# Softmax with logits of the other sign and the sink as a 129th column; output projections by 512 columns

## The chip, the cores and the metric

One NeuronCore of a Trainium2 chip runs the whole program in one launch. The metric is the device time of that launch in microseconds (us); lower is better. Its engines are TensorE (PE, matmuls; its weight loads are listed as PEld), VectorE (DVE), ScalarE (ACT), GpSimd (POOL) and SyncE (SP, which here only issues DMAs). Each takes its instructions in one fixed order and waits at the first that isn't ready.

## The reference

A decoder trunk of two layers over 1,024 positions of width 1,024, in float32. Layer A is a gated DeltaNet with an output projection (2,048 x 1,024). One set of keys and values (4 heads of 64) is then computed, and layer B is an attention of 32 query heads over a window of 128 positions, with an output projection of the same size. What the change touches is the softmax of layer B, whose denominator has one more term, a learned sink for each head, and the two products `@ w_out`:

```
q = rms_norm(q, q_gain) * (64 ** -0.5)
logits = einsum("bnqkgd,bnskd->bnkgqs", q, k_band) + bias
logits = where(mask, logits, -inf)            # 128 of 256 keys of a band lie in the window
m = maximum(max(logits), sink)
p = exp(logits - m)
probs = p / (sum(p) + exp(sink - m))
o = einsum("bnkgqs,bnskd->bnqkgd", probs, v_band)
return (o * silu(z)) @ w_out
```

## The kernel before

Each float32 operand of a large product is split into a rounded part and a remainder (hi and lo), and a product is three matmuls: hi by hi, hi by lo, lo by hi. TensorE's order is that in which the code is written; the orders of DVE, ACT, POOL and SP are made by a scheduler from priorities.

**Weights.** They stream through `wraw`, two buffers of 512 KB. `take()` hands out the next weight and fetches the ones ahead; `weight()` lets SP issue the load, then has POOL copy it into `whi` (L150; for weights with a norm gain POOL multiplies the gain in, two L153, and ACT rounds, L155), and DVE forms the remainder `wlo` in two halves (L157). `weights()` yields the sources in the order of use.

**Output projection** (`out_proj`, called for layer A with `a_w_out` and for layer B with `b_w_out`). It goes over two halves of 512 positions, two halves `cp` of 512 output columns, and in each over the 16 slices k of 128 input rows, four by four (k4). The stationary operand is the transposed activation (`oh` its rounded part, `ol` its remainder), the moving one the weight. Four accumulators in PSUM, one for each 128 positions, take 48 products each. A weight tile holds four slices k of 256 columns, so each accumulator is filled in two halves b. `tick()` counts steps: small pieces of other work, such as the transposes of the next norm (L239, which need the normed rows `xo` of DVE's L232), are written into PE's order at given ticks (`later(15, ...)` for the first half). `og_load` loads the next rows of activations, and DVE's L895 forms their remainder `ol`.

**Attention** (`b_attend`, between the projections). There are 64 blocks: 8 groups of 4 heads, each with 8 blocks of 128 queries. For block i PE's order has, in turns with the matmuls of the following groups' q and z products (L971 to L973 and L180 to L184): `turn(i)`, the transposes of its probabilities (L1192); `q_turn(i + 3)`; `logits(i + 2)`; `values(i - 1)`. So the softmax of a block has about the time of two blocks on PE before its `turn`. `logits` lets PE form the products with the keys (L1166, L1167), DVE put the window's 128 logits together (L1168), add the bias and take the running maximum from the sink on (L1172), negate it (L1176) and subtract it from the sink (L1178); ACT takes the exp of the sink's term (L1179) and of the logits, with their sum (L1182); DVE adds the sink's term (L1184) and inverts (L1185); POOL multiplies (L1186). POOL also makes the rounded queries (L1137) and masks the transposed probabilities (L1197), DVE norms the queries (L1103 among others).

## Time and profile before

| | |
|---|---|
| median of 3 runs | 1890.71 us (1887.74 to 1893.08) |
| profiled execution, its own time | 1894.54 us |
| span of its instructions | 1892.8 us |
| mean granted TensorE clock | 0.995 |
| busy: PE, DVE, ACT, POOL | 97%, 65%, 44%, 27% |

The profile is taken from one execution; its time lies a little above the median of the runs. The stages that the change touches are the projection of layer A (899 to 1089 us of the span), the attention (1170 to 1704) and the projection of layer B (1704 to 1893). Matmuls overlap, so the distance of two starts is what a matmul costs in a stream, not its own duration. The granted clock is given as a share of full speed: 1.00 is 2.4 GHz, 0.50 is 1.2 GHz.

### The profile page before, as it was taken

The page shows a single profiled execution, that of the slowest core. Times are in us where ns is not written, and L with a number is a line of the kernel's source. Part 1 is how long each engine was busy: PE and PEld are TensorE (multiplying, and loading weights), DVE is VectorE, ACT ScalarE, POOL GpSimd, SP SyncE. Part 2 cuts the span into 40 slices and gives each one's busy share as a digit, 9 for nine tenths or more (in the row PEclk, how much of TensorE's full clock was granted, in tenths as well). Part 3 has the DMA queues.
Part 4 walks back from the last instruction along what each step waited for, and adds up shares of the span by engine and source line. Part 5 has one row for each costly group of instructions (what it writes and reads, how often), then busy time and mean ns, then how long its engine had stood idle before and what let it go on. Part 6 is the DMA issues. An engine that isn't in the chain of part 4 may idle for free.

```text
span 1892.8 us, 34012 instructions
## 1 busy us (share of the span) xinstructions
PE 1829.7 (97%) x13186; PEld 1567.2 (83%) x13186; DVE 1239.6 (65%) x3014; ACT 838.1 (44%) x1968; POOL 512.6 (27%) x581
## 2 busy tenths in 40 slices
PE   6999999999999998999999999999999999999999
PEld 5667777787878776778999999888788788879999
DVE  6677776868595878765545366787776776753432
ACT  6446353635445364423011043656756666771100
POOL 0222222322232223221211232333433333321211
PEclk9999999999999999999999999999999999999999
DMA  4611111111111111133654321111211111226542
GB/s 149 143 37 34 56 45 57 34 56 46 34 57 34 46 34 58 33 96 99 229 182 152 112 90 46 42 38 46 67 32 48 56 49 43 73 73 200 188 166 82
DMA packets 151270, 149.74 MB, mean 79 GB/s; under 512 B 7242, under 2 KB 124484, under 8 KB 151108
## 3 DMA queue, kind: packets, MB, share of 16 engines
q1 hardware_dynamic: 140768, 130.40, 22.2%
q10 hardware_dynamic: 10340, 17.16, 2.9%
q8 instruction: 104, 1.70, 0.4%
q14 instruction: 58, 0.48, 0.1%
HBM read 116.05 MB, written 31.49 MB: 78 GB/s over the span
## 4 chain that ended last, share of the span: by engine, by line
PE 68%; DVE 13%; issue 5%; ACT 4%; POOL 3%; DMA 1%; POOLq 0%; ACTq 0%; SPq 0%; DVEq 0%
PE mm L182 8%; PE mm L180 8%; PE mm L184 8%; PE acc L920 6%; PE acc L919 6%; PE acc L921 6%; PE mm L971 4%; PE mm L973 3%; PE mm L972 3%; DVE acc L494 3%; PE pv L1213 2%; DVE wlo L157 2%; PE tp L1192 1%; PE kqp L666 1%; PE lg L1167 1%
## 5 line engine op out<-in xcount | busy, mean ns | idle before, releaser
L180 PE MATMUL mm<-hh,whi 128*128 128x512 f32 (+1 forms) x1040 | 427.2, 411 | 2.6 <-ACT hh L246 2.5
L182 PE MATMUL mm<-hl,whi 128*128 128x512 f32 (+1 forms) x1040 | 417.3, 401 | 1.6 <-DVE hl L247 1.5
L184 PE MATMUL mm<-hh,wlo 128*128 128x512 f32 (+1 forms) x1040 | 415.1, 399 | 0.0
L157 DVE TENSOR_TENSOR wlo<-wraw,whi 128x512 fp32r<-128x512 f32 x292 | 210.8, 749 | 239.4 <-POOL whi L150 214.0
L150 POOL TENSOR_SCALAR whi<-wraw 128x1024 fp32r<-128x1024 f32 x110 | 121.8, 1107 | 493.2 <-PE acc L921 248.3
L180 PEld LDWEIGHTS mm<-hh,whi 128*128 128x128 f32 x1040 | 197.5, 190 | 38.1 <-issue 4.6
L184 PEld LDWEIGHTS mm<-hh,wlo 128*128 128x128 f32 x1040 | 197.1, 190 | 36.0 <-issue 4.2
L182 PEld LDWEIGHTS mm<-hl,whi 128*128 128x128 f32 x1040 | 197.5, 190 | 34.6 <-issue 4.2
L971 PE MATMUL mm<-whi,hh 128*128 128x256 f32 x608 | 179.9, 296 | 0.0
L494 DVE SCALAR_TENSOR_TENSOR acc<-u,cw,acc 128x512 f32<-128x512 f32 x192 | 160.8, 839 | 23.5 <-POOL acc L491 21.0
L973 PE MATMUL mm<-whi,hl 128*128 128x256 f32 x608 | 171.8, 283 | 0.0
L972 PE MATMUL mm<-wlo,hh 128*128 128x256 f32 x608 | 171.7, 282 | 0.0
L919 PE MATMUL acc<-whi,hh 128*128 128x256 f32 x512 | 145.0, 283 | 0.0
L920 PE MATMUL acc<-wlo,hh 128*128 128x256 f32 x512 | 144.9, 283 | 0.0
L921 PE MATMUL acc<-whi,hl 128*128 128x256 f32 x512 | 144.9, 283 | 0.0
L971 PEld LDWEIGHTS mm<-whi,hh 128*128 128x128 f32 x608 | 115.6, 190 | 10.9 <-issue 10.8
L1182 ACT ACTIVATE lsb<-lsb,nm 128x128 f32<-128x128 f32 x256 | 99.8, 392 | 54.6 <-DVE se L1178 44.4
L972 PEld LDWEIGHTS mm<-wlo,hh 128*128 128x128 f32 x608 | 115.8, 190 | 0.2
L973 PEld LDWEIGHTS mm<-whi,hl 128*128 128x128 f32 x608 | 115.5, 190 | 0.0
L920 PE MATMUL acc<-wlo,oh 128*128 128x256 f32 x384 | 108.7, 283 | 1.2 <-DVE wlo L157 1.2
L919 PE MATMUL acc<-whi,oh 128*128 128x256 f32 x384 | 108.6, 283 | 0.0
L921 PE MATMUL acc<-whi,ol 128*128 128x256 f32 x384 | 108.5, 283 | 0.0
(355 smaller groups left out, 4207.0 us busy)
## 6 DMA issues: line engine op xcount, KB each, us to landing
wraw<-in_a_w_in SPq DMA_DIRECT2D x48, 512.0 KB, 4.0
wraw<-in_a_w_out SPq DMA_DIRECT2D x32, 512.0 KB, 4.2
wraw<-in_b_w_in SPq DMA_DIRECT2D x32, 512.0 KB, 4.0
wraw<-in_b_w_out SPq DMA_DIRECT2D x32, 512.0 KB, 3.9
og<-zs SPq DMA_DIRECT2D x32, 256.0 KB, 2.0
ogT<-zs SPq DMA_DIRECT2D x24, 256.0 KB, 2.1
btab<-lt SPq DMA_DIRECT2D x1, 4096.0 KB, 24.2
dm<-gd SPq DMA_DIRECT2D x8, 512.0 KB, 3.7
```

Of the source, the lines that this page charges most:

```text
L150: nc.gpsimd.tensor_scalar(out=hi, in0=raw, scalar1=1.0, scalar2=1.0, op0=ALU.mult, op1=ALU.mult)
L157: nc.vector.tensor_tensor(out=lo[:, ks], in0=raw[:, ks], in1=self.f32(hi[:, ks]), op=ALU.subtract)
L180: nc.tensor.matmul(ps, hi[:, k, :], hh[:, k, :], start=(k == 0), stop=False)
L182: nc.tensor.matmul(ps, hi[:, k, :], hl[:, k, :], start=False, stop=False)
L184: nc.tensor.matmul(ps, lo[:, k, :], hh[:, k, :], start=False, stop=(k == KT - 1))
L494: nc.vector.scalar_tensor_tensor(out=acc, in0=u[:, t:t + 512], scalar=cw[:, t, blk:blk + 1], in1=acc, op0=ALU.mult, op1=ALU.add)
L919: nc.tensor.matmul(po, oh[:, kk, ts], hi[:, kk, :], start=(k4 + kk + b == 0), stop=False)
L920: nc.tensor.matmul(po, oh[:, kk, ts], lo[:, kk, :], start=False, stop=False)
L921: nc.tensor.matmul(po, ol[:, kk, ts], hi[:, kk, :], start=False, stop=(k4 + kk + b == 7))
L971: nc.tensor.matmul(ps, hh[:, k, ts], hi[:, k % 4, :], start=(k == 0), stop=False)
L972: nc.tensor.matmul(ps, hh[:, k, ts], lo[:, k % 4, :], start=False, stop=False)
L973: nc.tensor.matmul(ps, hl[:, k, ts], hi[:, k % 4, :], start=False, stop=(k == KT - 1))
```

## The change

In the softmax, keys, bias and sinks are taken with the other sign (the keys by their gain, the bias by a factor in the copy of its table, the sinks by one instruction at the start, the mask's value too). The running maximum becomes a minimum m, which serves as the exp's bias as it is, with a scale of -1. The tile of logits gets a 129th column, into which POOL copies the negated sinks (L1160 of the changed kernel), so that the exp's own sum holds the sink's term; the negation, the difference, the extra exp and the sum on DVE go. In the projections a weight tile holds two slices k of 512 columns in place of four of 256, an accumulator is filled as one, and 768 matmuls of 512 columns take the place of 1,536 of 256 in each of them. The count of ticks stays.

```diff
-                ps = [acc.tile([P, 2, 256], F32, name="acc") for _ in range(4)]
+                ps = [acc.tile([P, 512], F32, name="acc") for _ in range(4)]
...
-                            po = ps[c][:, b, :]
-                            for kk in range(4):
-                                nc.tensor.matmul(po, oh[:, kk, ts], hi[:, kk, :], start=(k4 + kk + b == 0), stop=False)
-                                nc.tensor.matmul(po, oh[:, kk, ts], lo[:, kk, :], start=False, stop=False)
-                                nc.tensor.matmul(po, ol[:, kk, ts], hi[:, kk, :], start=False, stop=(k4 + kk + b == 7))
-                                if kk % 2:
-                                    self.tick()
+                            for kk in range(2):
+                                k = 2 * b + kk
+                                nc.tensor.matmul(ps[c], oh[:, k, ts], hi[:, kk, :], start=(k4 + k == 0), stop=False)
+                                nc.tensor.matmul(ps[c], oh[:, k, ts], lo[:, kk, :], start=False, stop=False)
+                                nc.tensor.matmul(ps[c], ol[:, k, ts], hi[:, kk, :], start=False, stop=(k4 + k == 6))
+                                self.tick()
...
+        nc.vector.tensor_scalar(out=sink, in0=sink, scalar1=-1.0, scalar2=None, op0=ALU.mult)
...
-        nc.vector.scalar_tensor_tensor(out=kg, in0=kg, scalar=64 ** -0.5, in1=qg, op0=ALU.mult, op1=ALU.mult)
+        nc.vector.scalar_tensor_tensor(out=kg, in0=kg, scalar=-(64 ** -0.5), in1=qg, op0=ALU.mult, op1=ALU.mult)
...
-        nc.scalar.copy(out=bk, in_=ps[0:32, 0:256])
+        nc.scalar.activation(out=bk, in_=ps[0:32, 0:256], func=AF.Copy, scale=-1.0)
...
-            L = Ls[i] = bp.tile([P, 4, P], F32, name="lsb", bufs=3)
+            L = Ls[i] = bp.tile([P, 4, P + 1], F32, name="lsb", bufs=3)
+            nc.gpsimd.tensor_copy(L[:, :, P:P + 1], sk.unsqueeze(2))
...
-                    nc.vector.tensor_tensor_reduce(out=L[:, e, :], in0=ps[:, j, P:256], in1=X.bias[:, e, :],
-                                                   scale=1.0, scalar=sk[:, e:e + 1], op0=ALU.add, op1=ALU.max,
+                    nc.vector.tensor_tensor_reduce(out=L[:, e, 0:P], in0=ps[:, j, P:256], in1=X.bias[:, e, :],
+                                                   scale=1.0, scalar=sk[:, e:e + 1], op0=ALU.add, op1=ALU.min,
                                                    accum_out=m[:, e:e + 1])
-            nm = sb.tile([P, 4], F32, name="nm")
-            nc.vector.tensor_scalar(out=nm, in0=m, scalar1=-1.0, scalar2=None, op0=ALU.mult)
-            se = sb.tile([P, 4], F32, name="se")
-            nc.vector.tensor_tensor(out=se, in0=sk, in1=m, op=ALU.subtract)
-            nc.scalar.activation(out=se, in_=se, func=AF.Exp)
             den = sb.tile([P, 4], F32, name="den")
             for e in range(4):
-                nc.scalar.activation(out=L[:, e, :], in_=L[:, e, :], func=AF.Exp, bias=nm[:, e:e + 1],
+                nc.scalar.activation(out=L[:, e, :], in_=L[:, e, :], func=AF.Exp, bias=m[:, e:e + 1], scale=-1.0,
                                      accum_out=den[:, e:e + 1])
-            nc.vector.tensor_tensor(out=den, in0=den, in1=se, op=ALU.add)
             nc.vector.reciprocal(den, den)
-            nc.gpsimd.tensor_tensor(out=L, in0=L, in1=den.unsqueeze(2).broadcast_to([P, 4, P]), op=ALU.mult)
+            p = L[:, :, 0:P]
+            nc.gpsimd.tensor_tensor(out=p, in0=p, in1=den.unsqueeze(2).broadcast_to([P, 4, P]), op=ALU.mult)
...
         for _ in range(2):
-            for c in (0, 2):
-                for k in range(4):
-                    for b in range(2):
-                        yield four(rows("a_w_out"), k, c + b, None)
+            for c in (0, 512):
+                for k in range(0, 16, 2):
+                    yield rows("a_w_out")[:, k:k + 2, c:c + 512], [2, 512], None
```

Outside the projections PE's order is the same as before. The scheduler's orders of the other engines move. Three places follow.

DVE at the start of layer A's projection: the remainders of weights (`wlo`) and of the activations' next rows (`ol`, from the loaded `kt` and `dm`), before:

```order
L157 TENSOR_TENSOR wlo<-wraw,whi 128x512 x3
L895 TENSOR_TENSOR ol_9472<-kt,oh_9471 128x1024
L895 TENSOR_TENSOR ol_9472<-dm,oh_9471 128x1024
L157 TENSOR_TENSOR wlo<-wraw,whi 128x512 x3
L895 TENSOR_TENSOR ol_9482<-kt,oh_9481 128x1024
L895 TENSOR_TENSOR ol_9482<-dm,oh_9481 128x1024
L157 TENSOR_TENSOR wlo<-wraw,whi 128x512 x11
```

and now:

```order
L157 TENSOR_TENSOR wlo<-wraw,whi 128x512 x3
L895 TENSOR_TENSOR ol_9473<-kt,oh_9472 128x1024
L895 TENSOR_TENSOR ol_9473<-dm,oh_9472 128x1024
L157 TENSOR_TENSOR wlo<-wraw,whi 128x512 x4
L895 TENSOR_TENSOR ol_9483<-kt,oh_9482 128x1024
L895 TENSOR_TENSOR ol_9483<-dm,oh_9482 128x1024
L157 TENSOR_TENSOR wlo<-wraw,whi 128x512 x10
```

One half of a weight's remainder has moved in front of the last pair of L895.

POOL in the attention around block 48: gain multiplications of a weight (`wraw`), the multiplications of the softmax (`lsb` by `den`; the ones shown belong to blocks 47 and 48), the masks (`pT`) and the rounded queries (`qh`), before:

```order
L153 TENSOR_TENSOR wraw<-wraw,gcolb 128x512 x2
L1197 AFFINE_SELECT pT_17362<-pT_17362 128x512
L1137 TENSOR_SCALAR qh<-qr 128x4x64
L1186 TENSOR_TENSOR lsb<-lsb,den 128x512
L1137 TENSOR_SCALAR qh<-qr 128x4x64
L153 TENSOR_TENSOR wraw<-wraw,gcolb 128x512 x2
L1186 TENSOR_TENSOR lsb<-lsb,den 128x512
```

and now, where the multiplication is L1182 and the copy of the sinks L1160 (the last L1182 shown is that of block 49):

```order
L153 TENSOR_TENSOR wraw<-wraw,gcolb 128x512 x2
L1160 COPY lsb<-sink 128x4
L1193 AFFINE_SELECT pT_16355<-pT_16355 128x512
L1137 TENSOR_SCALAR qh<-qr 128x4x64
L1182 TENSOR_TENSOR lsb<-lsb,den 128x4x128 x2
L1160 COPY lsb<-sink 128x4
L1193 AFFINE_SELECT pT_16453<-pT_16453 128x512
L1137 TENSOR_SCALAR qh<-qr 128x4x64
L153 TENSOR_TENSOR wraw<-wraw,gcolb 128x512 x2
L1160 COPY lsb<-sink 128x4
L1182 TENSOR_TENSOR lsb<-lsb,den 128x4x128
```

The second pair of gain multiplications stood in front of block 48's multiplication and stands behind it now. All over the attention, 6 multiplications stood directly behind a gain multiplication before; 19 now do, with at most a copy of the sinks between.

DVE at the first block of the attention: the norm of the queries (L1103), the logits (L1172, listed as ISA) and the inverse of the sum (`den`), before:

```order
L1103 TENSOR_TENSOR qr<-qr,rqby 128x1024
L1172 ISA lsb,m<-lg,bias,sink 128x128
L1172 ISA m 128x1
L1184 TENSOR_TENSOR den<-den,se 128x4
L1172 ISA lsb,m<-lg,bias,sink 128x128
L1172 ISA m 128x1
L1185 RECIPROCAL den<-den 128x4
```

and now, with the logits as L1173 and the inverse as L1180:

```order
L1180 RECIPROCAL den<-den 128x4
L1173 ISA lsb,m<-lg,bias,sink 128x128
L1173 ISA m 128x1
L1103 TENSOR_TENSOR qr<-qr,rqby 128x1024
L1173 ISA lsb,m<-lg,bias,sink 128x128
L1173 ISA m 128x1
```

The inverse stood behind the norm and stands in front of it now.

## Rows read from the trace of the kernel before

**Rows 1.** The page's first part: busy time, share of the span, instructions.

```profile
PE 1829.7 (97%) x13186; PEld 1567.2 (83%) x13186; DVE 1239.6 (65%) x3014; ACT 838.1 (44%) x1968; POOL 512.6 (27%) x581
```

**Rows 2.** By stage: length, busy PE, PEld, DVE, ACT, POOL (instructions); clock, DMA share, GB/s.

```profile
899.00:1089.00 190.00, 188.10 (x1570) 187.69 (x1569) 85.58 (x122) 24.02 (x32) 41.56 (x37) 1.00 0.51 168
...
1170.00:1704.00 534.00, 526.24 (x3603) 440.52 (x3603) 383.57 (x1387) 349.48 (x943) 187.78 (x234) 0.99 0.17 52
1704.00:1893.00 189.00, 185.03 (x1542) 184.44 (x1538) 68.31 (x91) 14.16 (x16) 32.59 (x30) 1.00 0.49 159
```

**Rows 3.** Timeline of PE in layer B's projection: start, duration, instruction.

```profile
1849.75 0.28 PE L920 MATMUL acc<-wlo,hh 128*128 128x256 f32 x1
...
1852.15 0.28 PE L919 MATMUL acc<-whi,hh 128*128 128x256 f32 x1
```

**Rows 4.** Timeline of PE in layer A's products of 512 columns.

```profile
205.55 0.40 PE L182 MATMUL mm<-hl,whi 128*128 128x512 f32 x1
...
209.64 0.39 PE L182 MATMUL mm<-hl,whi 128*128 128x512 f32 x1
```

**Rows 5.** Timeline of PE in the attention's products of 512 columns.

```profile
1581.70 0.40 PE L180 MATMUL mm<-hh,whi 128*128 128x512 f32 x1
...
1582.86 0.40 PE L184 MATMUL mm<-hh,wlo 128*128 128x512 f32 x1
```

**Rows 6.** Timeline of PE, start of layer A's projection; in brackets: idle, releaser.

```profile
906.33 0.38 PE L920 MATMUL acc<-wlo,kq 128*128 128x256 f32 x1 [0.70 <-DVE wlo L157]
...
924.29 0.28 PE L919 MATMUL acc<-whi,oh 128*128 128x256 f32 x1
925.77 0.39 PE L920 MATMUL acc<-wlo,oh 128*128 128x256 f32 x1 [1.20 <-DVE wlo L157]
```

**Rows 7.** Timeline of DVE at the same place.

```profile
921.59 1.22 DVE L895 TENSOR_TENSOR ol<-kt,oh 128x1024 fp32r<-128x1024 f32 x1 [4.40 <-ACT oh L894]
923.05 1.23 DVE L895 TENSOR_TENSOR ol<-dm,oh 128x1024 fp32r<-128x1024 f32 x1 [0.23 <-ACT oh L894]
924.20 2.73 DVE L157 TENSOR_TENSOR wlo<-wraw,whi 128x512 fp32r<-128x512 f32 x3
```

**Rows 8.** Timeline between the halves of layer A's projection, DVE and PE.

```profile
1003.41 1.41 DVE L232 TENSOR_SCALAR xo<-xo,nrs4y 128x1024 f32<-128x1024 f32 x2
...
1004.92 0.60 PE L239 MATMUL tr<-cst,xo 128*128 128x128 f32 x4
```

**Rows 9.** Groups by line, 1170 to 1704: busy us, mean ns, idle before.

```profile
L1192 PE MATMUL tp<-cst,lsb 128*128 128x128 f32 x256 | 38.7, 273 | 5.9 <-POOL lsb L1186 5.9
...
L1176 DVE TENSOR_SCALAR nm<-m 128x4 f32<-128x4 f32 x64 | 14.1, 221 | 0.8
```

**Rows 10.** Timeline of PE: transposes of blocks 0 and 48.

```profile
1179.97 0.66 PE L1192 MATMUL tp<-cst,lsb 128*128 128x128 f32 x4 [1.28 <-POOL lsb L1186]
...
1575.84 0.66 PE L1192 MATMUL tp<-cst,lsb 128*128 128x128 f32 x4 [2.01 <-POOL lsb L1186]
```

**Rows 11.** Timeline of POOL ahead of block 22's transposes.

```profile
1355.87 2.04 POOL L153 TENSOR_TENSOR wraw<-wraw,gcolb 128x512 f32<-128x512 f32 x2 [3.06 <-DMA wraw<-in_b_w_in]
1357.86 1.04 POOL L1186 TENSOR_TENSOR lsb<-lsb,den 128x512 f32<-128x512 f32 x1
```

**Rows 12.** Busy time and granted clock (0.50 in both) of two stretches.

```profile
1173.80:1177.20 3.40, 3.40 (x17) 3.40 (x18) 3.40 (x14) 2.21 (x10) 2.04 (x2) 0.50 0.00 0
1576.60:1580.00 3.40, 3.40 (x12) 2.71 (x11) 1.11 (x3) 1.11 (x5) 0.41 (x1) 0.50 0.02 5
```

**Rows 13.** Timeline of DVE ahead of block 0's transposes.

```profile
1176.79 1.21 DVE L1103 TENSOR_TENSOR qr<-qr,rqby 128x1024 f32<-128x1024 f32 x1
```

**Rows 14.** Small instructions of POOL, groups by line.

```profile
L486 POOL COPY u<-u 128x3 f32<-128x3 f32 x32 | 7.7, 241 | 4.3 <-DVE acc L494 4.3
...
L1034 POOL MEMSET neg<- 128x1 f32 x1 | 0.1, 103 | 8.8 <-PE tr L239 8.8
```

**Rows 15.** Timeline of PE at the attention's start.

```profile
1171.43 0.36 PE L1166 MATMUL lg<-kh,qT 128*128 128x256 f32 x1 [0.92 <-DVE rqbt L118]
```

More of the change, by code (lines that the diff above doesn't have):

```diff
@@ L916, in out_proj @@
                             ts = slice(c * P, c * P + P)
[L917 to L923 removed]
+                            for kk in range(2):
[4 more added lines that the diff above has]
+                                self.tick()
                             if (k4, b) == (3, 1):
[L925 to L926 removed]
+                                nc.vector.tensor_tensor(out=xs[c][:, cs], in0=ps[c], in1=xs[c][:, cs], op=ALU.add)
                                 nc.sync.dma_start(dst[half * 4 + c][:, cs], xs[c][:, cs])
@@ L1033, in layer_b @@
         self.neg = bp.tile([P, 1], F32, name="neg", bufs=1)
-        nc.gpsimd.memset(self.neg, NEG)
+        nc.gpsimd.memset(self.neg, -NEG)
         X = self.groups
@@ L1191, in turn @@
             for e in range(4):
-                nc.tensor.transpose(out=ps[:, e, :], in_=L[:, e, :], identity=self.ident)
+                nc.tensor.transpose(out=ps[:, e, :], in_=L[:, e, 0:P], identity=self.ident)
             pTs[i] = {}
@@ L1373, in weights @@
         for _ in range(2):
-            for c in (0, 2):
-                for k in range(4):
-                    for b in range(2):
-                        yield four(rows("b_w_out"), k, c + b, None)
+            for c in (0, 512):
+                for k in range(0, 16, 2):
+                    yield rows("b_w_out")[:, k:k + 2, c:c + 512], [2, 512], None
     def dump(self, name, ap):
```

2 lines of the change are left out of this document (removed).

## The prediction

> **What bounds the kernel now.** Read the share of each engine first: TensorE (PE) is busy 97% of the span, DVE 65%, ACT 44%, POOL 27% [rows 1]. So nearly every microsecond that can be won is either fewer PE nanoseconds or one of PE's few waits, and the work that the softmax loses on DVE and ACT pays only where PE waits for its result. The table by stage then says where to look [rows 2]: the change works inside the two output projections (899 to 1089 and 1704 to 1893, PE busy all but 1.9 and 4.0 us) and the attention (1170 to 1704, all but 7.8 us). All other stages keep their instructions on PE in the order that they had.
>
> **The projections: fewer, wider matmuls.** Each projection issues 1,536 matmuls of 256 columns and will issue 768 of 512. In a stretch of the second one without a wait, 21 matmuls start from 1849.75 to 1852.15, 20 intervals of 0.120 us [rows 3]. What a 512-column matmul costs in a stream of its kind is shown by layer A: 18 intervals from 205.55 to 209.64, 0.2272 us each [rows 4]. The stream in the attention gives the other bound: five intervals from 1581.70 to 1582.86, 0.232 us [rows 5]. Two narrow ones cost 0.240, so a pair saves 12.8 ns by the one row and 8 ns by the other. Layer A's stretch is the likeness: one accumulator, three terms in turn, nothing else in between, as in the projections; the attention's stretch alternates with transposes and small matmuls. I take 0.2267 to 0.2272, that is 13.3 ns: 768 x 13.3 ns = **10.2 us for each projection** (8 ns would make it 6.1). Below, a pair cannot save less than nothing unless a wide matmul stalls, which no stretch of the trace shows.
>
> The Trainium skill ("TensorE: Matmul & The Clock Gate", section "Back-to-back issue gap") puts the distance of two starts at the columns over 2.4 GHz plus about 2.5 ns. By that rule a pair would save 2.5 ns and both projections together 3.8 us instead of 20.4. The trace differs from it at both widths (0.120 measured against 0.109, 0.227 against 0.216), so I go by the rows.
>
> **The weights of the projections.** A tile has 512 KB as before and serves 24 wide matmuls instead of 48 narrow ones. Its load, its rounding on POOL, its remainder on DVE and its count of tiles (32 for each) stay; only the time that it covers falls from 48 x 0.120 = 5.76 to 5.44 us. That is cover enough: in the second projection no matmul waits for a weight. At the start of the first, two do [rows 6]: at 906.33 for 0.70 us, and at 925.77, where the start comes 1.48 us after the one ahead instead of 0.12, 1.36 too late. Why the second is late is in DVE's queue [rows 7]: the remainder of the weight (the L157 that starts at 924.20) stands behind two L895, which form the remainder of attention rows whose loads came in only then (1.22 and 1.23 us). The new order of DVE moves one L157 in front of that pair of L895, so this wait should go: **-1.36**. The first wait is for a weight that is loaded at that time anyway; PE comes to it 24 pairs x 13.3 ns = 0.32 us earlier and so waits longer: **+0.32**. One cover gets thin: the transposes of the first half's norm (L239) start at 1004.92, and DVE's L232 has ended at 1003.41 + 1.41 = 1004.82 [rows 8]. They are taken at the 15th tick, ticks will come every 0.68 instead of 0.72 us, and the norm's own chain gets no shorter, so PE comes 0.6 us early: **+0.6**. First projection -10.2 - 1.36 + 0.32 + 0.6 = **-10.6**, second **-10.2**.
>
> **The attention: what is removed.** For each of 64 blocks three small DVE instructions go (L1176, 221 ns, is the dearest, so at most 64 x 3 x 0.22 = 42 us of DVE) and one small exp of ACT [rows 9]. All of it lies beside PE's stream, so by itself it is worth nothing on the path. It pays where PE's transposes of the probabilities (L1192) wait for POOL's multiplication: 5.9 us in all [rows 9], in five places of which the first and the last are shown, 1.28 us at block 0 and 2.01 at block 48 [rows 10] (blocks 22, 29 and 40 have the rest). Each costs some 0.16 us more than its bracket, since the matmul behind it restarts slowly, so 6.7 us in all: 1.44 at block 0 and 5.3 at the other four.
>
> Why they are late is POOL's queue, not the length of the softmax [rows 11]. At block 22 the multiplication L1186 starts at 1357.86, right at the end of two gain multiplications of a weight (L153, 2.04 us), and these had sat 3.06 us in front of it until the weight's load came in; at blocks 29, 40 and 48 it stands likewise behind an L153. In the new order of POOL the pair that was in front of block 48 stands behind block 48's multiplication, and the same holds at blocks 22, 29 and 40. So I take these four waits as gone: **-5.3**. With them goes the clock drop behind the longest: after 2.01 us without work PE ran at 0.50 of full speed, 1.2 GHz, for 3.40 us from 1576.60 [rows 12], which did 1.7 us of work: **-1.7**. At block 0 the wait is DVE's: L1103 (1.21 us, started 1176.79) stood in front of the reciprocal [rows 13], in the new order it stands behind it: **-1.44**.
>
> **What is added there.** Sixty-four copies of four columns on POOL. The nearest rows are a copy of three columns, 241 ns, and a memset of one, 103 ns [rows 14]: 6.6 to 15.4 us on an engine that is busy 188 of 534 us, so I cost it at nothing on the path, with the block's exps, queued behind the copy, as the ones who would be late. The cover is that the copy needs only a free tile. The exp of 129 instead of 128 columns, the one negation of the sinks at the start, and the multiplication over rows of 129 I cost at nothing too (off the path). But the new order also puts more multiplications right behind an L153 (or an L153 and a copy): 19 of 64 blocks, where it was 6. Those six cost 5.3 us, 0.88 each on the mean. Most of the 19 stand behind weights that are issued early; I choose two as late: **+1.8**. Attention: -5.3 - 1.7 - 1.44 + 1.8 = **-6.6**.
>
> **Sum.** -10.6 - 10.2 - 6.6 = -27.4 us. The profiled execution (1894.54, its span 1892.8) would be 1867.1; it lies 3.8 above the median of the runs shown, so from 1890.7 the forecast is **1863.3 us**.
>
> **Rivals.**
> - *The softmax gives nothing* (16%): POOL's new order loses at other blocks what it wins at those four and at block 0. For it speaks that 19 multiplications now stand behind an L153. Only the projections are left: -20.8, **1870**.
> - *A wide matmul costs 0.232 us here* (10%), as in the attention: 1,536 x 8 = 12.3 us in place of 20.4, so -19.3, **1871**.
> - *The wide matmul saves nothing* (4%): two narrow ones at 0.240 already run at the array's rate and the 13 ns are of layer A's stream alone. Only the waits are left, -27.4 + 20.4 = -7.0, **1884**. The Trainium skill's rule on the gap (named above) is near to this case: by its 2.5 ns it would be 1880.
> - *All waits go* (8%): no new wait in the attention or at the norm (1.8 + 0.6), and its start-up gets smooth as well, with the first wait there (0.92 us [rows 15]) and the clock drop at 1173.80 (1.7 us [rows 12]) gone: -32.4, **1858**. Against it: that wait is for DVE's work on q's norm, which isn't shortened.
> - *POOL's order is bad* (5%): all 19 wait 0.88 us, 16.7 us, and the clock drop stays: -20.8 - 1.44 - 5.3 + 16.7 = -10.8, **1880**.
> - *Slower* (2%): matmuls that fill a whole accumulator stall. It takes 0.240 + 7.0 / 1536 = 0.2446 us for one to eat up the rest of the change; at 0.250 it would be +15.4 - 7.0 = +8.4, **1899**. Against it are [rows 4, 5], which fill a whole one.
>
> **How the numbers follow.** The forecast has 55%, with a range of its own of 1857 to 1870 (the waits of the attention between none gone and all gone, the runs' own spread). The range of 8 in 10 reaches down to the case in which all waits go and up past the two cases at 1870 and 1871: 1855 to 1876. A measurement of this kernel tells some 0.3%, 5.7 us, from no change: every case but the last is faster by more, and the one at 1884 just so, which leaves 95% faster, 3% within, 2% slower.
>
> **What would show it.** Right: starts of L919 to L921's successors 0.227 us apart; a weight tile every 5.44 us; the stages at 179.4, 178.8 and 527.4 us; no wait near 925; L1192's waits below 3 us in sum; no clock drop behind block 48. Wrong: gaps of 0.232 or 0.240 in the projections; transposes that wait behind an L153 at blocks that did not wait before; exps that wait for POOL's copy; a wait of PE for a weight in the middle of a projection.

## The result, and the profile after

The changed kernel takes 1869.02 us (median of 4 runs, 1865.79 to 1871.96) where the one before takes 1891.89: 22.9 us less, a ratio of 0.9882 (95% interval 0.9858 to 0.9906). The profiled execution has a span of 1866.1 us, 26.7 less than before; the profiled execution of before lay 2.7 us above its median and this one 1.2 us below, hence the two figures.

The page's first part for the changed kernel: PE still bounds it, with 1,536 instructions fewer.

```profile
PE 1810.6 (97%) x11650; PEld 1486.6 (80%) x11650; DVE 1219.4 (65%) x2823; ACT 834.8 (45%) x1904; POOL 527.9 (28%) x645
```

Where did the time go? The stages of [rows 2] move with the clock of the run, so both kernels are cut at the same events here: first to last matmul of layer A's projection, first logits to first matmul of layer B's projection, first to last matmul of that. The columns are those of [rows 2]. Before:

```profile
899.51:1089.58 190.07, 188.17 (x1570) 187.76 (x1569) 86.01 (x123) 24.15 (x31) 41.05 (x37) 1.00 0.51 168
1167.58:1704.46 536.88, 529.12 (x3626) 443.02 (x3625) 385.99 (x1391) 351.01 (x945) 188.31 (x235) 0.99 0.17 52
1704.46:1888.75 184.29, 184.29 (x1538) 184.29 (x1536) 67.61 (x90) 14.02 (x15) 32.59 (x30) 1.00 0.49 160
```

After:

```profile
898.83:1081.25 182.42, 181.67 (x803) 147.14 (x801) 86.22 (x123) 24.20 (x31) 40.73 (x37) 1.00 0.52 174
1159.27:1687.90 528.63, 526.59 (x3625) 442.43 (x3624) 369.44 (x1199) 348.19 (x882) 204.40 (x296) 1.00 0.18 55
1687.90:1861.90 174.00, 174.00 (x770) 144.11 (x768) 66.18 (x90) 13.81 (x15) 31.44 (x30) 1.00 0.48 164
```

Layer A's projection gained 7.65 us (forecast 10.6), the attention 8.25 (6.6), layer B's projection 10.29 (10.2); the other 0.5 us lie mostly in layer A ahead of its projection. In the attention DVE lost 16.5 us of busy time and POOL got 16.1 more, and PE is busy for all but 2.0 us of it.

The two projections do not pay the same for a wide matmul. PE's timeline, starts of the weight tiles in layer A (24 matmuls from one row to the next) and then of two in layer B:

```profile
933.32 0.39 PE L919 MATMUL acc<-whi,oh 128*128 128x512 f32 x1
...
938.92 0.40 PE L919 MATMUL acc<-whi,oh 128*128 128x512 f32 x1
...
944.39 0.40 PE L919 MATMUL acc<-whi,kq 128*128 128x512 f32 x1
...
950.01 0.39 PE L919 MATMUL acc<-whi,kq 128*128 128x512 f32 x1
...
1693.48 0.39 PE L919 MATMUL acc<-whi,hh 128*128 128x512 f32 x1
...
1698.92 0.39 PE L919 MATMUL acc<-whi,hh 128*128 128x512 f32 x1
```

In layer B a tile takes 5.44 us, 0.2267 a matmul, the row of layer A's products [rows 4]. In layer A two tiles of three take 5.60 and 5.62 (0.2333 and 0.2342) and the third 5.47 (0.2279), in a fixed cycle through the stage: 0.2318 in the mean, the other row [rows 5]. In place of 13.3 ns a pair saves 240 - 231.8 = 8.2 ns there, 768 times: 6.3 us.

The waits that answer to [rows 6, 7], PE's and DVE's timeline at the start of layer A's projection:

```profile
905.66 0.51 PE L920 MATMUL acc<-wlo,kq 128*128 128x512 f32 x1 [0.75 <-DVE wlo L157]
...
912.52 3.34 DVE L157 TENSOR_TENSOR wlo<-wraw,whi 128x512 fp32r<-128x512 f32 x4 [0.94 <-POOL whi L150]
919.11 1.23 DVE L895 TENSOR_TENSOR ol<-kt,oh 128x1024 fp32r<-128x1024 f32 x1 [3.25 <-ACT oh L894]
920.65 1.23 DVE L895 TENSOR_TENSOR ol<-dm,oh 128x1024 fp32r<-128x1024 f32 x1 [0.32 <-ACT oh L894]
922.82 3.32 DVE L157 TENSOR_TENSOR wlo<-wraw,whi 128x512 fp32r<-128x512 f32 x4 [0.94 <-POOL whi L150]
```

The wait near 925 is gone, since the remainder that PE needed, the fourth of those from 912.52 on, is formed ahead of the pair of L895. The first wait stays, about as long as before.

And all that PE waits for in the attention (table of waits: total, times, longest), where [rows 9] had 5.9 us for POOL:

```profile
PE lg L1167 <- DVE rqbt L118: 0.9, 1, 0.9
PE lg L1167 <- DVE m L1173: 0.8, 1, 0.8
PE tp L1146 <- DVE qh L1139: 0.3, 1, 0.3
```

No transpose of the probabilities waits for POOL any more (nor in t_after, a second traced execution of this kernel), and the clock stays up where the drop of [rows 12] was; the drop behind the start-up is still there. Length, busy times and granted clock (the third number from the end) of the two stretches:

```profile
1166.00:1169.00 3.00, 3.00 (x16) 3.00 (x16) 3.00 (x14) 0.92 (x4) 2.09 (x3) 0.50 0.00 0
1560.00:1570.00 10.00, 10.00 (x66) 8.19 (x65) 3.64 (x14) 6.98 (x18) 3.70 (x6) 1.00 0.24 76
```

What the prediction did not see is in one block of the softmax. Before, in steady state (timeline of DVE, ACT and POOL; the last logits matmul of the block starts at 1454.70, rows of the reductions between first and last left out):

```profile
1456.08 0.35 DVE L1172 CUSTOM_DVE_ANT_0 lsb<-lg,bias,sink 128x128 f32<-128x128 f32 x1
...
1456.89 0.34 DVE L1172 CUSTOM_DVE_ANT_0 lsb<-lg,bias,sink 128x128 f32<-128x128 f32 x1
...
1457.76 0.16 DVE L1176 TENSOR_SCALAR nm<-m 128x4 f32<-128x4 f32 x1
...
1458.01 0.40 ACT L1182 ACTIVATE lsb<-lsb,nm 128x128 f32<-128x128 f32 x1 [1.31 <-DVE se L1178]
...
1459.28 0.39 ACT L1182 ACTIVATE lsb<-lsb,nm 128x128 f32<-128x128 f32 x1
...
1460.49 2.10 POOL L1186 TENSOR_TENSOR lsb<-lsb,den 128x512 f32<-128x512 f32 x1 [6.05 <-DVE rqby L119]
```

and after (the last logits matmul starts at 1443.39):

```profile
1444.04 0.35 DVE L1173 CUSTOM_DVE_ANT_0 lsb<-lg,bias,sink 128x128 f32<-128x128 f32 x1
...
1444.85 0.35 DVE L1173 CUSTOM_DVE_ANT_0 lsb<-lg,bias,sink 128x128 f32<-128x128 f32 x1
...
1444.49 0.40 ACT L1178 ACTIVATE lsb<-lsb,m 128x129 f32<-128x129 f32 x1 [0.32 <-DVE m L1173]
...
1445.69 0.39 ACT L1178 ACTIVATE lsb<-lsb,m 128x129 f32<-128x129 f32 x1
...
1446.46 1.04 POOL L1182 TENSOR_TENSOR lsb<-lsb,den 128x512 f32<-128x512 f32 x1 [4.74 <-DVE rqby L111]
```

The one negation took the maxima of four heads, so the first exp could not start before the last head's reduction and the negation behind it: 1.93 us after the first reduction's start (in this block 0.6 us of them pass with another DVE instruction that stands between the two). Without it the first exp starts 0.45 us after it, while DVE reduces the second head. Over the 64 blocks, the time from the end of the last reduction to the end of the last exp fell from 3.00 to 1.36 us (medians), and the transposes start 5.46 us after the end of POOL's multiplication instead of 3.07 (means). From the last logits matmul to the end of the multiplication a block takes 6.5 us instead of 9.5 (medians). The 2.10 us of the multiplication in the block of before are an exception: the 64 take 1.07 in the mean.

### The profile page after: what moved, and what is told of

Read it like the earlier page. It is cut to its first block, busy times and chain, and to the rows that moved or that the text cites. A ratio compares the mean times of both kernels' runs of the same rounds, so it can differ in the third digit from the quotient of the medians.

```text
span 1866.1 us, 30785 instructions
## 1 busy us (share of the span) xinstructions
PE 1810.6 (97%) x11650; PEld 1486.6 (80%) x11650; DVE 1219.4 (65%) x2823; ACT 834.8 (45%) x1904; POOL 527.9 (28%) x645
## 3 DMA queue, kind: packets, MB, share of 16 engines
q1 hardware_dynamic: 124384, 130.40, 22.3%
## 4 chain that ended last, share of the span: by engine, by line
PE 76%; DVE 10%; issue 4%; POOL 3%; ACT 1%; DMA 0%; POOLq 0%; ACTq 0%; DVEq 0%
PE mm L182 9%; PE mm L180 9%; PE mm L184 9%; PE acc L920 6%; PE acc L921 6%; PE acc L919 6%; PE mm L971 4%; PE mm L972 4%; PE mm L973 4%; PE pv L1209 3%; DVE acc L494 3%; PE lg L1168 2%; PE lg L1167 2%; PE tp L1188 1%; DVE wlo L157 1%
## 5 line engine op out<-in xcount | busy, mean ns | idle before, releaser
L150 POOL TENSOR_SCALAR whi<-wraw 128x1024 fp32r<-128x1024 f32 x110 | 119.8, 1090 | 482.7 <-PE acc L921 242.8
L1178 ACT ACTIVATE lsb<-lsb,m 128x129 f32<-128x129 f32 x256 | 101.0, 397 | 71.3 <-DVE m L1173 42.8
L153 POOL TENSOR_TENSOR wraw<-wraw,gcolb 128x512 f32<-128x512 f32 x72 | 84.0, 1187 | 111.2 <-DMA wraw<-in_b_w_in 62.6
L1182 POOL TENSOR_TENSOR lsb<-lsb,den 128x512 f32<-128x512 f32 x64 | 69.3, 1082 | 154.1 <-DVE den L1180 134.4
L491 POOL TENSOR_SCALAR acc<-u,cw 128x512 f32<-128x512 f32 x64 | 56.3, 880 | 182.1 <-ACT u L487 168.4
L919 PE MATMUL acc<-whi,hh 128*128 128x512 f32 x256 | 99.7, 389 | 0.0
L921 PE MATMUL acc<-whi,hl 128*128 128x512 f32 x256 | 99.6, 389 | 0.0
L920 PE MATMUL acc<-wlo,hh 128*128 128x512 f32 x256 | 99.6, 389 | 0.0
```

Of the source, the lines that this page charges most:

```text
L150: nc.gpsimd.tensor_scalar(out=hi, in0=raw, scalar1=1.0, scalar2=1.0, op0=ALU.mult, op1=ALU.mult)
L919: nc.tensor.matmul(ps[c], oh[:, k, ts], hi[:, kk, :], start=(k4 + k == 0), stop=False)
L920: nc.tensor.matmul(ps[c], oh[:, k, ts], lo[:, kk, :], start=False, stop=False)
L921: nc.tensor.matmul(ps[c], ol[:, k, ts], hi[:, kk, :], start=False, stop=(k4 + k == 6))
```

## The experiments

One profiled execution of each kernel is compared by the stages cut as above, the attention's length in the first place. "From block 3" is the part of the attention from the transposes of block 3 on, without the start of the stage, which differs from kernel to kernel. "Ahead" tells at which of the blocks 22, 29, 40 and 48 POOL's order has the gain multiplications of a weight, which before stood ahead of the block's own multiplication, still ahead of it. "Margin" is the mean time from the end of POOL's multiplication to the start of the block's transposes, over 64 blocks; "tail" the median from the end of the last reduction to the end of the last exp. In the text, timed runs are given with the median of before on the same chip.

The time of v1_sign is that of experiment 11 (t_sign), "one" stands for a single run.

| kernel | attention, us | from block 3 | margin | tail | ahead | PE's waits for POOL there | time, us |
|---|---|---|---|---|---|---|---|
| before | 536.9 | 501.5 | 3.07 | 3.00 | all four | 5.9 in 5 | 1891.9 |
| the changed kernel | 528.6 | 494.5 | 5.46 | 1.36 | none | none | 1869.0 |
| e1_proj: projections alone | 536.6 | 501.3 | 3.08 | 3.00 | all four | 5.9 in 5 | 1876.3 |
| e2_soft: softmax alone | 527.8 | 494.5 | 5.26 | 1.14 | none | 0.8 in 1 | 1887.8 |
| v1_sign: no 129th column | 530.0 | 494.4 | 4.33 | 1.44 | none | 1.5 in 1 | 1868.2 |
| v2_col: no change of sign | 535.5 | 498.7 | 3.09 | 2.89 | 22, 48 | 5.7 in 4 | 1874.9 (one) |
| v3_dead: removed work put back | 542.2 | 505.4 | 2.48 | 3.07 | all four | 9.7 in 9 | 1882.4 (one) |
| v4_copy: softmax of before and copies | 541.2 | 504.3 | 2.32 | 3.15 | all four | 11.1 in 10 | 1883.3 (one) |
| v5_free: the same, copies into a spare tile | 540.4 | 505.1 | 2.47 | 3.04 | all four | 9.1 in 9 | 1877.5 (one) |
| e12_four: four negations | 535.3 | 495.3 | 3.77 | 1.83 | none | 0.2 in 1 | 1875.6 |

**1. The projections alone (e1_proj)**: the first two and the last hunk of the diff, for both weights; the softmax of before.

> Only the projections at 512 columns, the softmax as before. If the two parts of the change add up, the profile shows layer A's projection about 7.7 us and layer B's 10.3 us shorter than before, the attention as before with its 6.7 us of late transposes and the clock drop behind block 48, and the time is 18 us (0.95%) below before. If the projections' gain needs the new softmax (shared queues of POOL, DVE and SP), one of the two stages gains less than half of that.

1876.27 us against 1891.12, a ratio of 0.9922 (0.9908 to 0.9936): 14.8 us. The stages are 182.4, 536.6 and 174.0 us, so by the profile 7.6 and 10.3 us in the projections, and the attention as before with the waits at the same five blocks. The stages add up. (The time gained less than their 18 us, since the profiled execution of before lies 3.4 us above this median.)

**2. The softmax alone (e2_soft)**: the other hunks, with 256 columns.

> Only the softmax changed, the projections with 256 columns. If the parts add up, the attention alone gets shorter, by 8.2 us (0.45%): the waits of the transposes for POOL gone, no clock drop behind block 48; both projections within 0.5 us of before. If the attention's gain in the changed kernel came from the projections' new weight order (other loads, other queue), the waits at blocks 22, 29, 40 and 48 are still there and the time is that of before.

1887.81 us against 1891.12: 3.3 us between the medians, and 4.0 by the ratio, 0.9979 (0.9970 to 0.9987). The attention takes 527.8 us, 9.0 less than before, so its gain needs no wide matmuls. One wait of a transpose for POOL is left, 0.8 us at block 0; the same softmax has none there in the changed kernel. But layer B's projection takes 186.1, 1.8 more: one wait of PE for a weight, which before had none there.

```profile
1710.32 0.38 PE L920 MATMUL acc<-wlo,hh 128*128 128x256 f32 x1 [1.57 <-DVE wlo L157]
```

With the wide matmuls that wait does not show. The rest of the missing gain, 1.4 us between layer A's projection and the attention, is a clock drop near 1098 that some executions have and others not. By the ratios the timed parts add up to 14.8 + 4.0 = 18.8 us where the whole has 22.3; the intervals and this wait cover the difference.

**3. Other places in SBUF for the weights (e3_place).**

```diff
-        hi = view(pool.tile([P, 1024], F32R, name="whi"))
-        lo = view(pool.tile([P, 1024], F32R, name="wlo"))
+        hp, lp, ln = pool if isinstance(pool, tuple) else (pool, pool, "wlo")
+        hi = view(hp.tile([P, 1024], F32R, name="whi"))
+        lo = view(lp.tile([P, 1024], F32R, name=ln))
...
-                self.wpools, self.wcount, self.depth = [self.wsp], 0, 1
+                wq = pool(c1, "wq", 2, side="right")
+                self.wpools, self.wcount, self.depth = [wq], 0, 1
```

In layer A's projection the list of pools gives two tiles of three a `whi` in the pool `wx` (131 to 139 KB of the partition) and everything else a place in `wsp` (28 to 45 KB). The activations lie at 155 to 221 KB there, and at 45 to 110 KB in layer B's projection, whose weights go to 213 to 229 KB.

> The changed kernel with weights at other places of SBUF: in layer A's projection the rounded weight of two tiles in three lies in the high pool and all remainders in the low one; in layer B's projection all weights from the third tile on lie in a high pool. If the place of the weight decides between 0.227 and 0.233 us for a matmul of 512 columns, the starts behind matmuls with a high rounded weight in layer A's projection take 0.228 in the mean and those behind low ones 0.233, whichever tile of the three it is; and layer B's projection leaves its 0.2267 (for 0.230 or more, about 3 us in all). If it is the traffic of the stage (loads, other engines), both projections keep their means of 0.2317 and 0.2267.

PE's timeline in layer B's projection of this kernel, where L920 to L922 are the three matmuls:

```profile
1849.72 0.39 PE L920 MATMUL acc<-whi,hh 128*128 128x512 f32 x1
...
1853.00 0.39 PE L922 MATMUL acc<-whi,hl 128*128 128x512 f32 x1
```

Fourteen intervals in 3.28 us, 0.2343 each (the same over 702 starts), where the same code with low weights has 0.2267. In layer A's projection the distance behind a matmul with a high weight, when the next one's is high too, is 0.2293 (153 starts), and with low weights on both sides 0.2332 (240); where they alternate, 0.2329 and 0.2315. So the place decides, not the traffic of the stage, though mixed neighbours don't split as cleanly as expected. (The longer time of this kernel, 1880.7, comes from a wait of 3.9 us for a weight's remainder and a clock drop at the start of layer B's projection besides.)

**4. Near or far (e9_mid)**: as the second half of experiment 3, with the pool at 127 to 143 KB, just above the activations.

```diff
-                self.wpools, self.wcount, self.depth = [self.wsp], 0, 1
+                wq = pool(c1, "wq", 2)
+                self.wpools, self.wcount, self.depth = [wq], 0, 1
```

> The changed kernel with the weights of layer B's projection, from the third tile on, at 127 to 143 KB of the partition, right above the activations (45 to 110 KB) instead of below them (28 to 45 KB). In the run with the weights at 213 to 229 KB the starts were 0.2343 us apart, in the changed kernel 0.2267. If the distance of the two operands decides, this run is near 0.2267, since they are as close as before; if it is a border between a lower and an upper part of SBUF that lies below 127 KB, it is 0.232 or more, as far above.

```profile
1849.79 0.40 PE L920 MATMUL acc<-wlo,hh 128*128 128x512 f32 x1
...
1853.05 0.40 PE L919 MATMUL acc<-whi,hh 128*128 128x512 f32 x1
```

Again 14 intervals, in 3.26 us: 0.233. Nearness alone does not give the fast rate; a border between 110 and 127 KB would fit all five placements of the projections, with 0.227 to 0.228 where moving and stationary operand lie on one side of it. It does not fit the attention of the kernel before: with the moving operand at 45 to 110 KB its starts are 0.2318 us apart for weights at 28 to 45 KB [rows 5] and 0.2319 for weights at 127 to 143 KB (means of 249 and 259). So it is no rule beyond these streams.

**5. The column without the sign (v2_col).** The cut shows the softmax; the signs of keys, bias, sinks and mask and the maximum go back with it.

```diff
+            nm = sb.tile([P, 4], F32, name="nm")
+            nc.vector.tensor_scalar(out=nm, in0=m, scalar1=-1.0, scalar2=None, op0=ALU.mult)
...
-                nc.scalar.activation(out=L[:, e, :], in_=L[:, e, :], func=AF.Exp, bias=m[:, e:e + 1], scale=-1.0,
+                nc.scalar.activation(out=L[:, e, :], in_=L[:, e, :], func=AF.Exp, bias=nm[:, e:e + 1],
```

> The changed kernel with the sink as a 129th column but keys, bias and sinks of the old sign: one negation on DVE stays, the difference, the extra exp and the sum are gone. POOL's order has the multiplications of blocks 22 and 48 directly behind a gain multiplication, those of 29 and 40 not. If POOL's queue makes the transposes late, they wait at blocks 22 and 48 (about 0.8 and 2.0 us, with the clock drop behind 48, attention 4 to 5 us longer than in the changed kernel) and not at 29 and 40. If the shorter softmax makes them timely, there is no wait at any of the four and the attention is as long as in the changed kernel.

The waits in the timeline of PE (L1188 are the transposes; blocks 0, 7, 22 and 48):

```profile
1172.04 1.12 PE L1188 MATMUL tp<-cst,lsb 128*128 128x128 f32 x4 [2.66 <-POOL lsb L1182]
...
1229.81 0.66 PE L1188 MATMUL tp<-cst,lsb 128*128 128x128 f32 x4 [0.38 <-POOL lsb L1182]
...
1353.07 0.66 PE L1188 MATMUL tp<-cst,lsb 128*128 128x128 f32 x4 [0.50 <-POOL lsb L1182]
...
1567.84 0.66 PE L1188 MATMUL tp<-cst,lsb 128*128 128x128 f32 x4 [2.16 <-POOL lsb L1182]
```

At 22 and 48, and not at 29 and 40, as the queue theory had it, and at 7, which stands behind a gain multiplication in this order as well. Its tail is nearly that of before, so at 29 and 40 the change of order was enough to end the wait. Apart from the signs this kernel differs from the changed one by a single DVE instruction for each block, of some 0.2 us, and its attention is 6.9 us longer: with that instruction POOL's order moves too.

**6. The sign without the column (v1_sign)**, which puts back the difference, the exp and the sum, and takes POOL's copies away.

```diff
-            L = Ls[i] = bp.tile([P, 4, P + 1], F32, name="lsb", bufs=3)
-            nc.gpsimd.tensor_copy(L[:, :, P:P + 1], sk.unsqueeze(2))
+            L = Ls[i] = bp.tile([P, 4, P], F32, name="lsb", bufs=3)
...
+            se = sb.tile([P, 4], F32, name="se")
+            nc.vector.tensor_tensor(out=se, in0=m, in1=sk, op=ALU.subtract)
+            nc.scalar.activation(out=se, in_=se, func=AF.Exp)
...
+            nc.vector.tensor_tensor(out=den, in0=den, in1=se, op=ALU.add)
```

> The changed kernel without the 129th column: keys, bias and sinks of the other sign, so no negation, but the difference, the extra exp and the sum on DVE stay, and POOL copies no sinks. POOL's order is nearly that of the changed kernel (blocks 22, 40 and 48 not behind a gain multiplication). If POOL's queue decides, there are no waits of the transposes at 22, 40 and 48 in spite of the longer softmax, and the attention takes 528 to 530 us. If the length of the softmax decides, they are back and it takes 534 us or more.

530.0 us. Of the transposes' waits one is left, at block 0:

```profile
PE tp L1191 <- POOL lsb L1185: 1.5, 1, 1.5
```

So the negation is nearly the whole gain in the attention, and the first case of the expectation came true: the order of the changed kernel, no waits at 22, 40 and 48, 528 to 530 us. The second case is wrong in its picture: without the negation this softmax is not longer but shorter than before, by the tail. So the run does not tell order and length apart.

**7. The removed work put back as dead work (v3_dead)**: a copy of m read by the exps, the difference and its exp, and a multiplication by one.

```diff
+            nm = sb.tile([P, 4], F32, name="nm")
+            nc.vector.tensor_scalar(out=nm, in0=m, scalar1=1.0, scalar2=None, op0=ALU.mult)
+            se = sb.tile([P, 4], F32, name="se")
+            nc.vector.tensor_tensor(out=se, in0=m, in1=sk, op=ALU.subtract)
+            nc.scalar.activation(out=se, in_=se, func=AF.Exp)
...
-                nc.scalar.activation(out=L[:, e, :], in_=L[:, e, :], func=AF.Exp, bias=m[:, e:e + 1], scale=-1.0,
+                nc.scalar.activation(out=L[:, e, :], in_=L[:, e, :], func=AF.Exp, bias=nm[:, e:e + 1], scale=-1.0,
...
+            nc.vector.tensor_scalar(out=den, in0=den, scalar1=1.0, scalar2=None, op0=ALU.mult)
```

> The changed kernel with dead work of the removed kind added (a copy of the minimum in place of the negation, the difference, its exp, a multiplication of the sum by one): the same result by a softmax as long as before. POOL's order comes out with blocks 22, 29, 33, 38, 40 and 48 behind a gain multiplication, as before. By the queue the waits are back at 22, 29, 40 and 48 (0.5 to 2.2 us each, the clock drop behind 48) and the attention takes 535 to 537 us; if the order made no difference but the length did, it would be the same here, so this run tells only against a third cause (the sign, the column, the POOL copy themselves), by which it would take 528 us.

542.2 us: longer than before by 5.3, which neither theory had. Nine waits, at 22, 29, 40 and 48 as the queue had it (0.4 to 2.1 us), at block 0, and at 16, 20, 21 and 33, which had none before:

```profile
PE tp L1194 <- POOL lsb L1188: 9.7, 9, 2.5
```

**8. The copies alone (v4_copy)**: the softmax of before in a tile of 129 columns, and

```diff
+            nc.gpsimd.tensor_copy(L[:, :, P:P + 1], sk.unsqueeze(2))
```

> The projections of the changed kernel and the softmax of before, with nothing added but POOL's copy of the sinks into a 129th column that nobody reads. POOL's order has the same blocks behind a gain multiplication as before. If the copies lie beside the path, as forecast, the attention takes what it took with the softmax of before (536.6 us in the run with the projections alone, within 1 us); if they cost POOL time that its waiters see, more waits than before and 538 us or more.

541.2 us, 4.7 more than the run with the projections alone. The forecast that the copies lie beside the path is wrong for a softmax of this length. In POOL's queue the copy waited 45 times and 117 us in sum for the transposes that free the tile of three blocks ago, which I had priced at nothing ("the copy needs only a free tile").

```profile
PE tp L1192 <- POOL lsb L1186: 11.1, 10, 3.6
...
PE tp L1192: 116.9, 45
```

**9. The same copies without that wait (v5_free).**

```diff
+            spare = sb.tile([P, 4, 1], F32, name="spare")
+            nc.gpsimd.tensor_copy(spare, sk.unsqueeze(2))
```

> As the run with the softmax of before and POOL's 64 copies of the sinks, but the copies go into a small tile of their own that nobody reads, so that none has to wait until the transposes of three blocks ago have freed the tile of logits. If that wait in POOL's queue is what cost 4.7 us, the attention is back at 536.6 us (within 1 us), with waits only at the blocks that had them before. If it is the copies' own time on POOL (12 us in all), it stays at 540 us or more.

540.4 us, still 3.8 above, with waits at much the same blocks as in experiment 8. So the wait for the tile is not the cause, and that theory of mine fell. By the wording of the expectation this would leave the copies' own time; but the scheduler's order of DVE, ACT and SP shifts with them too (from 93 us behind the first logits on, weight loads are issued 2.0 to 6.1 us later than in experiment 1), and the runs do not separate the two.

**10. Four negations instead of one (e12_four)**, on the kernel of experiment 1:

```diff
-            nm = sb.tile([P, 4], F32, name="nm")
-            nc.vector.tensor_scalar(out=nm, in0=m, scalar1=-1.0, scalar2=None, op0=ALU.mult)
...
+                    nc.vector.tensor_scalar(out=nm[:, e:e + 1], in0=m[:, e:e + 1], scalar1=-1.0, scalar2=None,
+                                            op0=ALU.mult)
```

> The projections of the changed kernel and the softmax of before, signs, sink terms and all, but the negation of the four maxima as four instructions of one column, each right behind its head's reduction, in place of one of four columns behind all four. DVE has three more instructions for each block, not fewer. If the gain came from letting the first head's exp start before the last head's reduction is done (from the last reduction to the last exp 3.0 us with the one negation, 1.4 without it), that step falls to 2 us or less, the waits at blocks 22, 40 and 48 go and the attention takes 528 to 531 us. If it came from DVE having less to do, the attention takes 537 us or more.

The tail falls to 1.83 us and the waits for POOL go, all but 0.2 us, with three DVE instructions more in each block and nothing else changed in the softmax. So what costs is that one instruction joins four heads, not what DVE has to do. It is no test of the way, though, since POOL's order moved with it: the gain multiplications are no longer ahead at any of the four blocks. The attention's length did not follow, 535.3 us, which neither case had, because a new wait stands at its start: PE stood still for 5.9 us there, and the clock was at 0.50 for the 9 us around it. PE waited for a remainder of the queries (L1137) that DVE's order has at 1171.73 us, behind the norm of other queries; experiment 1 has it at 1165.66. From block 3 on the stage takes 495.3 us, 6.0 less than in experiment 1 and 0.8 more than in the changed kernel. Timed it is 1875.63 against 1889.89, 0.9924 (0.9907 to 0.9942), no better than experiment 1.

```profile
PE tp L1144 <- DVE nm L1174: 5.9, 1, 5.9
...
PE tp L1191 <- POOL lsb L1185: 0.2, 1, 0.2
```

```profile
1166.00:1175.00 9.00, 3.08 (x15) 2.79 (x16) 8.48 (x31) 3.53 (x15) 4.75 (x6) 0.50 0.01 4
```

**11. The changed kernel and the sign alone, timed together (t_after, t_sign).**

> The changed kernel itself once more, for a narrower interval beside the next run. By the profiles of the parts (18.3 us for the projections alone, 6.5 to 8 us for the softmax) it should be 1.2 to 1.4% faster than before; by the sum of the timed parts (14.8 and 4.0 us) 1.0%.

> The changed kernel without the 129th column (the sign alone). If the gain in the attention is that of the order of POOL's queue, and the removed sink terms and the added copies only matter at block 0 (1.5 us), it is 0 to 2.5 us slower than the changed kernel. If the shorter softmax counts in more places than the profiled look shows, it is over 4 us slower.

1868.48 us (0.9878, 0.9863 to 0.9892) and 1868.24 us (0.9883, 0.9864 to 0.9903) against 1892.48. The two can't be told apart: the 129th column, with its copies and without the sink terms, is worth nothing that the times show, neither way, and over 4 us is excluded; the profiles have 1.6 us for it, the wait at block 0. The 1.2% of the changed kernel lies between the 1.0% to which the parts timed in experiments 1 and 2 add up and the 1.4% of the profiles' stages (26.2 of 1892.8 us).

## Why the prediction was right, and where it was not

The time alone does not say that the forecast's case came true: 1869.0 is nearer to the rival "the softmax gives nothing" (1870). The profile decides between them, with 8.25 us gained in the attention where that rival has none. That the sum of the stages, -26.2 us, came so near to the forecast's is luck in part: layer A's projection fell short by 2.9 us and the attention gained 1.7 more.

The forecast was -27.4 us; measured were -22.9 and -24.0 between medians and -26.7 between the profiles, against which the terms were sized. Term by term, by the profiles:

- **Layer B's projection** (-10.2): -10.3. The row from layer A's products was the right likeness, and no weight is late.
- **Layer A's projection, the matmuls** (-10.2): about -6.3. The mechanism was right and the size off: the step "I take 0.2267 to 0.2272" gave both projections one price, and this one pays 0.2318, the price of the bound that was set aside. The rival at 0.232 was right for one projection of the two. Why: experiments 3 and 4. The trace of before had a hint that I did not follow up: 0.227 is found in layer A in stretches only (the mean of 1,543 starts there is 0.2303), and I took one of them for the whole.
- **Its waits** (-1.36 + 0.32 + 0.6): the wait at 925 is gone as forecast, the one at 906 grew by hardly anything, and no wait came at the norm. In the new order of DVE no L895 stands between the norm's small operations, where one of 1.23 us stood before; that is more than the 0.6 us that PE comes early. Together about -1.4.
- **The four waits and the clock drop in the attention** (-5.3 - 1.7): all gone, 7.1 us between the lengths from block 3 on. **Block 0** (-1.44): gone, with 1.2 us gained ahead of its transposes, where the start-up waits grew by 0.2; in experiment 2, with the same softmax, 0.8 us of it are left. **New waits** (+1.8): none.

The sentence "Why they are late is POOL's queue, not the length of the softmax" holds for these four waits. At block 48 of the kernel before, DVE's reciprocal and POOL's timeline are

```profile
1570.39 0.18 DVE L1185 RECIPROCAL den<-den 128x4 f32<-128x4 f32 x1
...
1572.22 2.05 POOL L153 TENSOR_TENSOR wraw<-wraw,gcolb 128x512 f32<-128x512 f32 x2 [3.98 <-DVE m L1172]
1574.23 1.55 POOL L1186 TENSOR_TENSOR lsb<-lsb,den 128x512 f32<-128x512 f32 x1
```

The sums were ready at 1570.57 us, and the multiplication started 3.7 us later, at the end of the pair of L153, whose weight had landed at 1572.06. At 22 and 40 it started 2.6 and 2.0 us behind its reciprocal, likewise at the end of an L153. With POOL's order as it was, and with weights that land when they did, earlier sums would have changed nothing at these three. Block 29 the prediction read too simply: the multiplication stands behind an L153 there too, but it started 0.71 us after that one's end and 0.14 us behind the reciprocal. The reciprocal stood in DVE's order behind an instruction (L1139) that had waited 1.78 us for POOL's L1137, itself behind an L153, so it was POOL's queue by a detour. In the changed kernel block 48's multiplication follows its reciprocal at once, with POOL idle before it:

```profile
1552.85 0.18 DVE L1180 RECIPROCAL den<-den 128x4 f32<-128x4 f32 x1 [0.92 <-ACT lsb L1178]
...
1553.11 1.04 POOL L1182 TENSOR_TENSOR lsb<-lsb,den 128x512 f32<-128x512 f32 x1 [3.59 <-DVE den L1180]
```

In every kernel of the table PE waits at one of the four blocks exactly where the column "ahead" has it, and v2_col has no wait at 29 and 40 with a tail like that of before.

What the prediction had wrong is the term of the new waits and, behind it, the price of the removed work: I had shortened the softmax by the durations of the removed instructions only. The negation cost 0.22 us and joined four heads: without it each exp follows its own reduction, and the last one ends 1.6 us earlier in each block. Every kernel whose exps need no joined instruction has the new order at all four blocks, and every kernel whose exps need one keeps the old order at two or four. So its removal is nearly the whole gain (experiments 6, 10 and 11), and at the four blocks the gain comes by way of the order that the scheduler makes. It also makes room: in the changed kernel POOL's queue still holds nine multiplications 0.6 to 2.4 us behind their reciprocals, all behind a gain multiplication, and their transposes start 2.6 us or more after the multiplication's end. That this room comes from the earlier sums, and that it is why none of the 19 made PE wait, is likely but not shown: no run has the whole order of the changed kernel with the old tail. The wait for the joined result stood in the page of before, in the group of the exps (busy time and mean ns of one, then the idle time ahead of them and what ended most of it):

```profile
L1182 ACT ACTIVATE lsb<-lsb,nm 128x128 f32<-128x128 f32 x256 | 99.8, 392 | 54.6 <-DVE se L1178 44.4
```

Forty-four of the 54.6 us end with the difference, the instruction right behind the negation on DVE. I had read these rows for their durations and not for what they wait for.

The second wrong step is the copies "at nothing". With the old softmax they cost 3.8 to 4.7 us (experiments 8 and 9); in the changed kernel nothing of this shows (experiment 11). Whether it is POOL's time or the order that moves with them stays open.

The Trainium skill's rule ("TensorE: Matmul & The Clock Gate", section "Back-to-back issue gap") would have the distance at 216 ns for 512 columns and a saving of 2.5 ns for each pair. That section calls the rule the gap of an isolated matmul, which the prediction left out, and gives 131 ns for 512 columns in a stream. Measured are 227 to 232 ns and 8.2 to 13.3; neither figure fits, and the measurements decide.

## What to carry to other kernels

An instruction that takes the results of several others at once costs more than its duration: it makes the first of them wait for the last. Before pricing its removal, draw the chain once with it and once without it, consumer by consumer. Where a scheduler makes the orders, an edit can gain through the order alone: look, for each wait, when the result was ready and when its consumer started, before the length of the chain is blamed. A price per matmul is to be taken from several stretches, and when they differ by 2% over hundreds of instructions, from one whose operands lie where those of the new stream will, if there is one. An instruction that is added to an in-order queue is not free because the engine has idle time; ask how much room its waiters have.

## What the runs showed of the hardware that was not expected

- **The place of the operands.** The same stream of 512-column matmuls runs at 0.2267 us with weights at 28 to 45 KB and activations at 45 to 110 KB, at 0.2333 with weights at 127 to 143 KB, and at 0.2343 with weights at 213 to 229 KB. With activations at 155 to 221 KB it runs at 0.228 for weights at 131 to 139 KB and at 0.2335 for weights at 28 to 45 KB. Matmuls of 256 columns took 0.118 to 0.120 in all places that the kernel before has for them. What makes the difference is not settled.
- **The runs' spread goes with the clock.** Of the changed kernel's four executions the spans are 1864.1, 1866.1, 1868.5 and 1870.2 us at mean granted clocks of 0.997, 0.996, 0.995 and 0.994. A thousandth of the clock is 1.9 us of this span, about what one stretch of some 3.4 us at half speed costs, so from one of them to the next it is about one such stretch more. Which of the waits bring one differs: in both traced executions of this kernel (after and t_after) PE waits 2.24 us near 715 us and 1.14 near 1090, and the clock then falls to 0.50 behind the first wait in the one and behind the second in the other.
